# The first tile's norm weights, applied per partition behind the transposes instead of along the rows ahead of them

## The chip, the cores and the metric

The kernel runs on one core of a Trainium2 chip. The metric is the device time of one launch in microseconds (us). The core has five engines that work side by side, each through its own instructions in order: TensorE (PE in the profile; its weight loads are PEld), VectorE (DVE), ScalarE (ACT), GpSimd (POOL) and SyncE (SP), which here issues nearly all the transfers (DMAs). They wait for each other by semaphores.

## What is computed

One layer with 512 rows of 1024 features. The input is normalized, multiplied by its weights `norm_mix_pre` and projected by `w_in`; the projections feed a recurrence and a sparse attention, and a feed-forward net follows. All of the change lies in the first two lines below and in the first columns of `z`.

```python
def rmsnorm(x, g):
    x32 = x.astype(jnp.float32)
    y = x32 * lax.rsqrt(jnp.mean(x32 * x32, axis=-1, keepdims=True) + NORM_EPS)
    return (y * g.astype(jnp.float32)).astype(x.dtype)

h = rmsnorm(x, norm_mix_pre[i])
z = h @ w_in[i]
xr, gr, q, kc, vc, ksl, vsl, kw, vw, g_nsa, gm_rnn, gm_attn = jnp.split(z, IN_SPLITS, axis=-1)
```

## The kernel before

Every 32-bit product is made of three: each operand is split into a high half that TensorE reads in one pass (`fp32r`) and the low rest, and high x high, high x low and low x high are summed in PSUM. ScalarE makes the high half (a cast), VectorE the low one (a subtraction). A split of a weight block is therefore one DMA, one cast and one subtraction.

The 512 rows are four tiles of 128. For each, `x_load` fetches the rows; ScalarE sums the squares; VectorE makes mean plus epsilon, GpSimd raises it to the power -0.5 (`rstd`), and VectorE multiplies the rows by it and by the weights `g_pre`, which stand as one row of 1024 in all 128 partitions (`xn`). `to_T` (L228) then turns `xn` on TensorE, eight blocks of 128x128, four to a PSUM bank, and splits each bank as a whole into `aTh` (ScalarE, L237) and `aTl` (VectorE, L238), features on the partitions.

`v_unit(t, br)` (L325) multiplies tile t by the weights `VWh`/`VWl`: 8 steps of 128 features, three matmuls each, so 24 matmuls of 256 columns (`br` 0, the unit's PSUM tile is `mm`) or of 304 (`br` 1, `sc`). The weights of `br` 0 come as two blocks of 2 steps (`vw_first`, tiles `raw`) and one of 4 steps (`vw_parts[0]`, staged in `y`), those of `br` 1 as four of 2 steps (also in `y`). `VP` lists which of these four are subtracted on GpSimd instead of VectorE. In the middle of the units stand the transposes of the next tile: `TV` says behind how many steps; for the first tile it is 12, that is behind 4 steps of the second unit.

For the first tile all is done by halves of 512 columns (`norm1_halves`, L300), and `g_pre` is made on the core: `spread` (L367) multiplies a column of ones by the weights' row (`g_row`, one partition, 4 KB), and ScalarE copies the two products into `g_pre`. `keep_warm(n)` (L362) issues n matmuls of 512 columns on a constant tile (`warm`), whose result nobody reads; `WARM` gives their numbers at four places: ahead of the product, behind it, and behind each half of the transposes.

Behind the units come the projections: `f_raw(n)` (L142) issues the DMA of weight block n (512 KB, tile `raw`), `f_split(n)` (L148) its cast (`wh`) and subtraction (`wl`). Blocks 0, 1 and 2 are loaded in the loop over the tiles (L405), blocks 0 and 1 split there too (L409); the split of block 2 is called for in the middle of the first projection (`proj_k`, L177), and nothing but the scheduler says where it goes.

The order of each engine's instructions is made by a scheduler, which sorts by its own estimates of when operands are there; TensorE's is kept as written (`strict`). `keep_in_program_order` and `issue_after` bind it at single places. The transfers are issued by SyncE and run one behind the other through 16 DMA engines.

Of the kernel before, what the change touches and what calls it, by code (L numbers as in the profile page):

```python
# [8 lines left out]
F32 = mybir.dt.float32  # L9
F32R = mybir.dt.float32r  # L10
BF16 = mybir.dt.bfloat16
AF = mybir.ActivationFunctionType
# [19 lines left out]
PRO = (22, 5, 0, 0, 1, 12, 4, 3)  # L32
TK = (1, 7, 1)
TV = (12, 7, 8, 11)
VP = (4,)
WARM = (7, 2, 1, 3)


def f32(ap):
    return ap.bitcast(F32)  # L40
# [3 lines left out]
def layer_kernel(ctx, tc, a, out):  # L44
# [18 lines left out]
    def bank(tag, shape=None):  # L63
        return ps.tile(shape or [128, 512], F32, tag=tag, name=nm(tag), bufs=PB[tag])
# [24 lines left out]

    def pe(ins):  # L90
        return tc.keep_in_program_order(ins) if strict[0] else ins

    def mm(*args, **kw):
        return pe(nc.tensor.matmul(*args, **kw))  # L94

    def tp(*args):
        return pe(nc.tensor.transpose(*args))  # L97
# [108 lines left out]
            next(filler[0], None)  # L206


    slcol = const.tile([128, NG], F32, name="slcol")
    for h in range(NH):  # L210
        nc.gpsimd.memset(slcol[32 * (h % 4):32 * (h % 4) + 32, h // 4:h // 4 + 1], SLOPE[h])
    ident = const.tile([128, 128], F32, name="ident")
    make_identity(nc, ident)
    mhalf = const.tile([128, 1], F32, name="mhalf")
    nc.gpsimd.memset(mhalf, -0.5)

# [8 lines left out]
        last["pow"] = nc.gpsimd.tensor_tensor(r, r, mhalf, op=OP.pow)  # L225
        return r

    def to_T(src, t, tag, then=None):  # L228

        for b in range(2):  # L230
            pt = bank(tag)
            for j in range(4):
                k = 4 * b + j
                tp(pt[:, j * 128:(j + 1) * 128], src[:, k * 128:(k + 1) * 128], ident)
            v = pt.rearrange("p (j q) -> p j q", j=4)
            oh = aTh[:, 4 * b:4 * b + 4, t * 128:(t + 1) * 128]
            last["Th"] = nc.scalar.copy(oh, v)  # L237
            last["Tl"] = nc.vector.tensor_sub(aTl[:, 4 * b:4 * b + 4, t * 128:(t + 1) * 128], v, f32(oh))  # L238
            if then:
                then(b)  # L240

    def bcast_row(pool, src, tag, bufs):
        g = pool.tile([128, D], F32, tag=tag, name=nm(tag), bufs=bufs)
# [33 lines left out]

    def vw_first(k, ks, w):
        raw = wraw(w_in[:, k:k + ks, C_VSL:C_VSL + 256], [128, ks, 256], w, 0)
        nc.scalar.copy(VWh[:, k:k + ks, 0:256], raw)  # L280
        nc.vector.tensor_sub(VWl[:, k:k + ks, 0:256], raw, f32(VWh[:, k:k + ks, 0:256]))

    def vw_load(parts):
        for c0, src, n, k, ks in parts:
# [9 lines left out]
    def x_load(t, parts=(slice(0, D),)):  # L294
        v = e1.tile([128, D], F32, tag="x", name=nm("x"), bufs=3)
        for c in parts:
            nc.sync.dma_start(v[:, c], a["x"][0, t * 128:(t + 1) * 128, c])
        return v

    def norm1_halves(v, then):  # L300
        xn = e1.tile([128, D], F32, tag="xn", name=nm("xn"))
        ss = e1.tile([128, 2], F32, tag="ss2", name=nm("ss"), bufs=1)
        for u, c in enumerate(HALF):
            nc.scalar.activation(xn[:, c], v[:, c], AF.Square, accum_out=ss[:, u:u + 1])
        then()
        r = e1.tile([128, 1], F32, tag="rstd", name=nm("rstd"), bufs=4)
        nc.vector.tensor_scalar(ss[:, 0:1], ss[:, 0:1], 1.0 / D, EPS, op0=OP.mult, op1=OP.add)
        nc.vector.scalar_tensor_tensor(r, ss[:, 1:2], 1.0 / D, ss[:, 0:1], op0=OP.mult, op1=OP.add)
        last["pow"] = nc.gpsimd.tensor_tensor(r, r, mhalf, op=OP.pow)
        for c in HALF:  # L310
            last["xn"] = nc.vector.scalar_tensor_tensor(xn[:, c], v[:, c], r, g_pre[:, c], op0=OP.mult, op1=OP.mult)
        return xn

    def norm1_sum(v):
        xn = e1.tile([128, D], F32, tag="xn", name=nm("xn"))
        ss = e1.tile([128, 1], F32, tag="ss", name=nm("ss"), bufs=4)
        nc.scalar.activation(xn, v, AF.Square, accum_out=ss)
        return v, xn, ss
# [34 lines left out]

    warm = e1.tile([128, S], BF16, name="warm", bufs=1)
    nc.vector.memset(warm, 1.0)
    ones = e1.tile([1, 128], F32, name="ones", bufs=1)
    nc.vector.memset(ones, 1.0)
    g_row = e1.tile([1, D], F32, name="g_row", bufs=1)
    nc.scalar.dma_start(g_row, a["norm_mix_pre"][0:1, :])
    g_pre = e1.tile([128, D], F32, name="gpre", bufs=1)  # L360

    def keep_warm(n):  # L362
        p_ = bank("sc")
        for i in range(n):
            mm(p_, warm[:, 0:128], warm, start=(i == 0), stop=(i == n - 1))

    def spread():  # L367
        keep_warm(WARM[0])
        pg = [bank("mm") for c in HALF]
        for c, p_ in zip(HALF, pg):  # L370
            mm(p_, ones, g_row[:, c], start=True, stop=True)
        keep_warm(WARM[1])
        for c, p_ in zip(HALF, pg):
            nc.scalar.copy(g_pre[:, c], p_)

    x0 = x_load(0, HALF)
    xn = norm1_halves(x0, spread)
    pow0 = last["pow"].ins
    with tc.issue_after(last["xn"].ins):
        vw_first(0, 2, "a")  # L380
    to_T(xn, 0, "tr", lambda b: keep_warm(WARM[2 + b]))
    with tc.issue_after(last["xn"].ins):
        vw_first(2, 2, "b")
    early = ExitStack()
    early.enter_context(tc.issue_after(last["Th"].ins))
    early.enter_context(tc.issue_after(last["Tl"].ins))
    vw_load(vw_parts[:1])
    xv = {1: norm1_sum(x_load(1))}
    vw_load(vw_parts[1:])

    def turn_next(t):
# [970 lines left out]
```

## Time and profile before

| | |
|---|---|
| median of 3 runs | 933.45 us (933.41 to 933.84) |
| the profiled execution, its own time | 935.22 us |
| its span, first to last instruction | 933.2 us |
| TensorE busy (PE) | 914.7 us, 98% of the span |
| VectorE (DVE) | 619.7 us, 66% |
| ScalarE (ACT) | 478.9 us, 51% |
| GpSimd (POOL) | 131.2 us, 14% |
| DMA, mean over the span | 101 GB/s |
| DMA in the first of 40 slices (0 to 23 us) | 279 GB/s |

Busy shares are means over stages with different limits. TensorE is nearly always busy, so a change in the first 25 us is read from the order of events there: which wait ends last ahead of a stretch without holes. In a chain or a timeline each line has the start in us, the length in us, the engine, the line of the kernel and what is written from what; a bracket at the end gives the idle time just before and the engine or DMA that ended it. Matmuls are pipelined, so of a row of them the distance of the starts is the price, not the length of one.

### The profile page before, as it was taken

To read this page: it belongs to the slowest core of one execution; us is meant where nothing else is said; L and a number is where in the kernel's file an instruction comes from. 1 tells how busy PE (TensorE), PEld (TensorE's weight loads), DVE (VectorE), ACT (ScalarE), POOL (GpSimd) and SP (SyncE) were. 2 spreads that over 40 slices of the span, in tenths; PEclk is the share of its full clock that TensorE was granted. 3 is DMA by queue.
4 is the path that set the end of the run, shared out by engine and by line. 5 is a ranking of instruction groups with operands and counts; after the bars stand their busy time and mean duration, and the time that the engine had idled before them with its cause. 6 is when DMAs were issued, how large, how long until landed. Compare 5 with 4: busy or idle time off the path is not lost.

```text
span 933.2 us, 12423 instructions
## 1 busy us (share of the span) xinstructions
PE 914.7 (98%) x4496; PEld 754.8 (81%) x4496; DVE 619.7 (66%) x1198; ACT 478.9 (51%) x878; POOL 131.2 (14%) x214
## 2 busy tenths in 40 slices
PE   8999999999999999999999999999999999989998
PEld 5988888878878878878788988888888888777786
DVE  6657785968788888787847444434334478988933
ACT  6456947566667767666745322232223244555610
POOL 4001201123243223333302000000000000000100
PEclk9999999999999999999999999999999999999999
DMA  9224344362123111201136133333333345516401
GB/s 279 79 75 123 97 121 128 95 132 68 46 55 82 46 46 46 68 27 65 65 133 187 48 89 90 102 102 91 95 108 91 92 147 199 190 61 218 166 34 46
DMA packets 123999, 94.04 MB, mean 101 GB/s; under 512 B 6081, under 2 KB 107297, under 8 KB 123938
## 3 DMA queue, kind: packets, MB, share of 16 engines
q1 hardware_dynamic: 122784, 91.16, 32.3%
q0 software_dynamic: 1152, 2.10, 1.4%
q8 instruction: 35, 0.57, 0.2%
q14 instruction: 26, 0.21, 0.1%
q10 hardware_dynamic: 2, 0.00, 0.0%
HBM read 89.05 MB, written 2.10 MB: 98 GB/s over the span
## 4 chain that ended last, share of the span: by engine, by line
PE 86%; DVE 9%; ACT 3%; issue 2%; POOL 0%; DVEq 0%; ACTq 0%
PE mm L94 44%; PE sc L94 23%; PE mq L94 6%; PE pv L94 5%; PE tr L94 5%; PE tr L97 4%; DVE e L787 1%; DVE PT L871 1%; DVE wl L156 1%; ACT e L790 1%; PE sc L97 1%; DVE att L901 1%; ACT wh L155 0%; DVE pc L852 0%; DVE r L600 0%
## 5 line engine op out<-in xcount | busy, mean ns | idle before, releaser
L94 PE MATMUL mm<-aTh,wh 128*128 128x512 f32 (+1 forms) x536 | 211.8, 395 | 0.6 <-ACT st L1105 0.6
L94 PE MATMUL mm<-aTh,wl 128*128 128x512 f32 (+1 forms) x536 | 206.2, 385 | 0.1
L94 PE MATMUL mm<-aTl,wh 128*128 128x512 f32 (+1 forms) x536 | 206.0, 384 | 0.2 <-DVE aTl L238 0.2
L94 PEld LDWEIGHTS mm<-aTh,wl 128*128 128x128 f32 x536 | 100.8, 188 | 20.9 <-DVE wl L156 0.5
L94 PEld LDWEIGHTS mm<-aTh,wh 128*128 128x128 f32 x536 | 100.8, 188 | 19.3 <-issue 2.7
L84 ACT CAST wh<-raw 128x1024 fp32r<-128x1024 f32 x43 | 45.3, 1054 | 135.2 <-PE mm L94 58.1
L94 PEld LDWEIGHTS mm<-aTl,wh 128*128 128x128 f32 x536 | 101.1, 189 | 16.4 <-DVE aTl L238 0.5
L802 POOL TENSOR_SCALAR e<-e,sm 128x128 f32<-128x128 f32 (+3 forms) x128 | 80.0, 641 | 153.8 <-DVE sm L798 107.4
L85 DVE TENSOR_TENSOR wl<-raw,wh 128x1024 fp32r<-128x1024 f32 x43 | 52.6, 1223 | 68.1 <-ACT wh L84 62.8
L156 DVE TENSOR_TENSOR wl<-raw,wh 128x1024 fp32r<-128x1024 f32 x59 | 73.6, 1248 | 30.7 <-ACT wh L155 29.8
L790 ACT ACTIVATE e<-e,mn 128x128 f32<-128x128 f32 (+3 forms) x128 | 71.3, 558 | 25.9 <-DVE mn L787 19.0
L94 PE MATMUL sc<-aTh,wh 128*128 128x512 f32 (+1 forms) x208 | 79.3, 381 | 0.0
L155 ACT CAST wh<-raw 128x1024 fp32r<-128x1024 f32 x59 | 61.9, 1050 | 34.0 <-PE mm L94 30.0
L94 PE MATMUL sc<-aTh,wl 128*128 128x512 f32 (+1 forms) x208 | 79.2, 381 | 0.0
L94 PE MATMUL sc<-aTl,wh 128*128 128x512 f32 (+1 forms) x208 | 79.2, 381 | 0.0
L787 DVE CUSTOM_DVE_ANT_0 e<-sc,toep 128x128 f32<-128x128 f32 (+3 forms) x128 | 59.5, 483 | 17.3 <-PE sc L94 16.4
L871 DVE TENSOR_TENSOR PT<-tr,PT 128x512 fp32r<-128x512 f32 x96 | 56.5, 596 | 15.4 <-ACT PT L870 14.4
L870 ACT CAST PT<-tr 128x512 fp32r<-128x512 f32 x96 | 47.5, 509 | 26.0 <-PE tr L97 25.3
L991 POOL TENSOR_TENSOR ss<-ss,ss 128x1 f32<-128x1 f32 x8 | 4.6, 577 | 392.6 <-ACT junk L979 392.6
L94 PE MATMUL sc<-KS,QS 128*128 128x512 f32 (+2 forms) x192 | 54.6, 366 | 1.1 <-DVE mn L787 1.0
L97 PE MATMUL tr<-ident,e 128*128 128x128 f32 x320 | 49.3, 273 | 2.9 <-DVE c L821 2.0
L97 PEld LDWEIGHTS tr<-ident,e 128*128 128x128 f32 x320 | 39.6, 140 | 13.0 <-PE tr L97 2.6
(360 smaller groups left out, 1762.4 us busy)
## 6 DMA issues: line engine op xcount, KB each, us to landing
raw<-in_w_in_dram SPq DMA_DIRECT2D x48, 512.0 KB, 3.6
raw<-in_ffn_w_gate_up_dram SPq DMA_DIRECT2D x44, 512.0 KB, 3.7
raw<-in_ffn_w_down_dram SPq DMA_DIRECT2D x30, 512.0 KB, 4.1
raw<-in_ple_w_gate_dram SPq DMA_DIRECT2D x8, 512.0 KB, 4.0
x<-in_x_dram SPq DMA_DIRECT2D x7, 512.0 KB, 7.0
raw<-in_w_out_dram SPq DMA_DIRECT2D x6, 512.0 KB, 3.6
raw<-in_cmp_k_w_dram SPq DMA_DIRECT2D x4, 512.0 KB, 3.7
raw<-in_cmp_v_w_dram SPq DMA_DIRECT2D x4, 512.0 KB, 3.9
```

The lines of the kernel that those rows point to most:

```text
L84: nc.scalar.copy(h, raw)
L85: nc.vector.tensor_sub(l, raw, f32(h))
L94: return pe(nc.tensor.matmul(*args, **kw))
L97: return pe(nc.tensor.transpose(*args))
L155: nc.scalar.copy(h, RAW[n])
L156: nc.vector.tensor_sub(l, RAW[n], f32(h))
L787: nc.vector.tensor_tensor_reduce(e[:, br, :], src, toep[:, 384 - 128 * i:S], SLOPE[h], BIG, op0=OP.add, op1=OP.min, accum_out=mn[:, u, br: ...
L790: tt(nc.scalar.activation(e[:, br, :], e[:, br, :], AF.Exp, scale=-1.0, bias=mn[:, u, br:br + 1], accum_out=sm[:, u, br:br + 1]))
L802: nc.gpsimd.tensor_scalar(ev, ev, sm[:, v, br:br + 1], 1.0, op0=OP.mult, op1=OP.mult)
L870: nc.scalar.copy(P[:, 0, :2 * n], pt[:, :2 * n])
L871: nc.vector.tensor_sub(P[:, 1, :2 * n], pt[:, :2 * n], f32(P[:, 0, :2 * n]))
L901: last["cl_dve"] = nc.vector.tensor_add(att[64 * u:64 * u + 64, half * 256:half * 256 + 256], pv[0:64, u, :], tmp[:, u, :])
```

## The change

The first tile's `xn` is now `x` times `rstd` alone (a `tensor_scalar` per half). The weights are loaded as eight rows of 128 (`g_rows`), turned by one transpose into a column per step (`g_col`, 128 partitions x 8), and applied where the turned tile leaves PSUM: `first_T` casts and subtracts each of the eight 128x128 blocks by itself, with that step's column as a scale per partition. `spread`, `ones` and `g_row` are gone. The constant matmuls stand at two places, 7 and 6 (`WARM = 13`), ahead of the transposes. The other tiles still use `g_pre`, which is now a broadcast load of 512 KB (`bcast_row`), issued behind the load of the second tile. `VP` is empty: all four subtractions of `br` 1 are VectorE's. `ident` is made ahead of `slcol`.

```diff
-VP = (4,)
-WARM = (7, 2, 1, 3)
+VP = ()
+WARM = 13
...
-            last["xn"] = nc.vector.scalar_tensor_tensor(xn[:, c], v[:, c], r, g_pre[:, c], op0=OP.mult, op1=OP.mult)
+            last["xn"] = kept(nc.vector.tensor_scalar(xn[:, c], v[:, c], r, None, op0=OP.mult))
...
-    g_row = e1.tile([1, D], F32, name="g_row", bufs=1)
-    nc.scalar.dma_start(g_row, a["norm_mix_pre"][0:1, :])
-    g_pre = e1.tile([128, D], F32, name="gpre", bufs=1)
+    g_rows = e1.tile([KT, 128], F32, name="g_rows", bufs=1)
+    nc.scalar.dma_start(g_rows, a["norm_mix_pre"][0].rearrange("(k p) -> k p", p=128))
+    g_col = e1.tile([128, KT], F32, name="g_col", bufs=1)
...
-    def spread():
-        keep_warm(WARM[0])
-        pg = [bank("mm") for c in HALF]
-        for c, p_ in zip(HALF, pg):
-            mm(p_, ones, g_row[:, c], start=True, stop=True)
-        keep_warm(WARM[1])
-        for c, p_ in zip(HALF, pg):
-            nc.scalar.copy(g_pre[:, c], p_)
+    def first_T(src):
+
+        for b in range(2):
+            pt = bank("tr")
+            for j in range(4):
+                k = 4 * b + j
+                tp(pt[:, j * 128:(j + 1) * 128], src[:, k * 128:(k + 1) * 128], ident)
+            for j in range(4):
+                k = 4 * b + j
+                v, oh = pt[:, j * 128:(j + 1) * 128], aTh[:, k, 0:128]
+                last["Th"] = kept(nc.scalar.activation(oh, v, AF.Copy, scale=g_col[:, k:k + 1]))
+                last["Tl"] = kept(nc.vector.scalar_tensor_tensor(aTl[:, k, 0:128], v, g_col[:, k:k + 1], f32(oh),
+                                                                 op0=OP.mult, op1=OP.subtract))
+            if b == 0:
+                vw_first(2, 2, "b")
 
     x0 = x_load(0, HALF)
-    xn = norm1_halves(x0, spread)
+    keep_warm(WARM - 6)
+    pg = bank("tr")
+    tp(pg[:, :KT], g_rows, ident[:KT, :KT])
+    kept(nc.vector.tensor_copy(g_col, pg[:, :KT]))
+    xn = norm1_halves(x0)
     pow0 = last["pow"].ins
+    keep_warm(6)
     with tc.issue_after(last["xn"].ins):
         vw_first(0, 2, "a")
-    to_T(xn, 0, "tr", lambda b: keep_warm(WARM[2 + b]))
-    with tc.issue_after(last["xn"].ins):
-        vw_first(2, 2, "b")
+        first_T(xn)
...
     xv = {1: norm1_sum(x_load(1))}
+    g_pre = bcast_row(e1, a["norm_mix_pre"][0], "gpre", 1)
     vw_load(vw_parts[1:])
```

Three places of the order that follows from it. ScalarE, from the first tile's transposes on, before (`L237` casts a bank of the turned tile, `L288` weights staged in `y`, `L317` sums squares, `L332` and `L335` take a unit's result, `L155` casts a projection's weight block; `wh61_592` is block 2's):

```order
L237 CAST aTh_91<-tr10_161 128x4x128
L237 CAST aTh_91<-tr12_170 128x4x128
L288 CAST VWh_117<-y_96 128x4x256
...
L317 ACTIVATE xn22_251,ss23_252<-x21_249 128x1024
L237 CAST aTh_91<-tr24_254 128x4x128
L237 CAST aTh_91<-tr25_261 128x4x128
...
L332 CAST V_106<-mm26_283 128x4x64
L155 CAST wh61_592<-raw46_476 128x1024
```

And now (`L374` casts one block of 128 columns with its scale, `L239` is the cast of a bank, `L157` that of a projection's block; `wh59_599` is block 2's; brackets name the semaphores waited for):

```order
L374 ACTIVATE aTh_91<-tr9_160,g_col_124 128x128 [waits DVE_49,PE_49]
L374 ACTIVATE aTh_91<-tr9_160,g_col_124 128x128 [waits DVE_49] x3
L280 CAST VWh_117<-raw10_173 128x2x256 [waits DMAHW4_49]
L374 ACTIVATE aTh_91<-tr11_177,g_col_124 128x128 [waits PE_49]
L374 ACTIVATE aTh_91<-tr11_177,g_col_124 128x128 [waits DVE_49] x3
L288 CAST VWh_117<-y_96 128x4x256 [waits DMAHW5_49]
...
L316 ACTIVATE xn20_258,ss21_259<-x19_256 128x1024 [waits DMAHW4_49]
L157 CAST wh59_599<-raw44_483 128x1024 [waits DMAHW0_49]
L239 CAST aTh_91<-tr22_261 128x4x128 [waits PE_49]
```

Two casts of a bank have become eight of a block, the later ones with a wait for VectorE, and the cast of block 2 has moved from behind the second tile's first unit to ahead of the second tile's transposed halves.

VectorE, from the weights of the second unit to the second tile's low halves, before:

```order
L290 TENSOR_TENSOR VWl_118<-y_96,VWh_117 128x2x304 x2
L322 SCALAR_TENSOR_TENSOR xn16_190<-x15_188,rstd20_245,gpre_126 128x1024
L290 TENSOR_TENSOR VWl_118<-y_96,VWh_117 128x2x304
L333 TENSOR_TENSOR V_106<-mm18_205,V_106 128x4x64
L224 TENSOR_SCALAR rstd27_305<-ss23_252 128x1
L322 SCALAR_TENSOR_TENSOR xn22_251<-x21_249,rstd27_305,gpre_126 128x1024
L238 TENSOR_TENSOR aTl_92<-tr24_254,aTh_91 128x4x128
```

and now:

```order
L290 TENSOR_TENSOR VWl_118<-y_96,VWh_117 128x2x304 [waits DMAHW3_49,Activation_49]
L332 TENSOR_TENSOR V_106<-mm16_212,V_106 128x4x64 [waits Activation_49]
L321 SCALAR_TENSOR_TENSOR xn13_195<-x12_193,rstd18_252,gpre15_198 128x1024 [waits DMAHW7_49,DMAHW6_49,Pool_49]
L226 TENSOR_SCALAR rstd25_312<-ss21_259 128x1 [waits Activation_49]
L158 TENSOR_TENSOR wl60_600<-raw44_483,wh59_599 128x1024 [waits DMAHW0_49,Activation_49]
L321 SCALAR_TENSOR_TENSOR xn20_258<-x19_256,rstd25_312,gpre15_198 128x1024 [waits DMAHW4_49,Pool_49]
L240 TENSOR_TENSOR aTl_92<-tr22_261,aTh_91 128x4x128 [waits Activation_49]
```

The second tile's `xn` has moved behind all four weight subtractions and the first unit's V, and block 2's subtraction to ahead of the second tile's `aTl`.

SyncE, the issues of the transfers from the load of the second tile on, now:

```order
L297 DMA x_193<-in_x_dram 128x1024
L244 DMA gpre_198<-in_norm_mix_pre_dram 128x1024
L287 DMA y<-in_w_in_dram 128x2x304 x4
L297 DMA x_256<-in_x_dram 128x1024
L297 DMA x_316<-in_x_dram 128x1024
L148 DMA raw_340<-in_w_in_dram 128x8x128
L148 DMA raw_397<-in_w_in_dram 128x8x128
L148 DMA raw_483<-in_w_in_dram 128x8x128
L429 DMA prow<-in_conv_w_dram 32x128
```

The broadcast (`gpre`) is new, and block 2 (`raw_483`) stands ahead of four loads for the recurrence (`y` from `lru_wa` and `lru_wx`), two of which were ahead of it.

## Rows read from the trace of the kernel before

**Rows 1.** The page: the chain that ended last, shares of the span by engine

```profile
PE 86%; DVE 9%; ACT 3%; issue 2%; POOL 0%; DVEq 0%; ACTq 0%
```

**Rows 2.** Waits of TensorE, 20 to 130 us: total, times, longest us

```profile
PE mm L94 <- DVE aTl L238: 0.6, 1, 0.6
```

**Rows 3.** The chain, 20 to 45 us: start us, length us, what

```profile
22.30 2.51 PE mm L94 x19
...
29.39 2.84 PE mm L94 x24
...
42.76 2.33 PE mm L94 x10
```

**Rows 4.** Windows: stretch, length, busy PE PEld DVE ACT POOL, clock, DMA share, GB/s

```profile
0.00:12.00 12.00, 10.55 (x24) 4.52 (x25) 4.24 (x9) 6.06 (x12) 6.37 (x32) 1.00 0.83 283
12.00:14.00 2.00, 2.00 (x12) 1.84 (x11) 1.67 (x2) 2.00 (x5) 0.00 (x0) 1.00 1.04 409
14.00:16.00 2.00, 2.00 (x18) 2.00 (x18) 1.65 (x4) 2.00 (x5) 1.66 (x3) 1.00 1.10 326
16.00:18.00 2.00, 1.56 (x12) 1.32 (x10) 2.00 (x2) 1.75 (x4) 2.00 (x2) 1.00 1.20 288
```

**Rows 5.** DMA issues at 16.7 and at 464.2 us: count, KB, us to landing

```profile
raw<-in_w_in_dram SPq DMA_DIRECT2D x1, 512.0 KB, 7.0
...
g<-in_norm_mix_post_dram SPq DMA_DIRECT2D x1, 512.0 KB, 8.8
```

**Rows 6.** Groups by form, whole span: count, busy us, mean ns, idle before

```profile
L155 ACT CAST wh<-raw 128x1024 fp32r<-128x1024 f32 x59 | 61.9, 1050 | 34.0 <-PE mm L94 30.0 <-PE sc L94 3.8
...
L544 ACT COPY KC<-tr 128x124 f32<-128x124 f32 x1 | 0.2, 243 | 0.0
...
L790 ACT ACTIVATE e<-e,mn 128x128 f32<-128x128 f32 x32 | 12.6, 395 | 5.6 <-DVE mn L787 5.4
...
L821 DVE SCALAR_TENSOR_TENSOR c<-ctab,tr 128x128 f32<-128x128 f32 x16 | 3.5, 278 | 0.3 <-PE tr L97 0.3
```

**Rows 7.** Timeline, 1 to 22 us: start, length, engine, line, operation

```profile
1.45 3.17 PE L94 MATMUL sc<-warm 128*128 128x512 bf16 x7 [1.45 <-DVE warm L355]
...
6.19 0.55 POOL L309 TENSOR_TENSOR rstd<-rstd,mhalf 128x1 f32<-128x1 f32 x1 [2.67 <-DVE rstd L308]
...
8.98 0.75 DVE L311 SCALAR_TENSOR_TENSOR xn<-x,rstd,gpre 128x512 f32<-128x512 f32 x1 [0.88 <-ACT gpre L374]
...
12.08 0.69 DVE L238 TENSOR_TENSOR aTl<-tr,aTh 128x512 fp32r<-128x512 f32 x1 [0.54 <-ACT aTh L237]
...
13.02 1.23 DVE L290 TENSOR_TENSOR VWl<-y,VWh 128x1024 fp32r<-128x1024 f32 x1 [0.25 <-ACT VWh L288]
...
14.66 1.49 DVE L290 TENSOR_TENSOR VWl<-y,VWh 128x608 fp32r<-128x608 f32 x2 [0.35 <-ACT VWh L288]
...
15.60 0.28 PE L94 MATMUL mm<-VWh,aTl 128*128 128x256 f32 x1
...
16.07 2.53 DVE L322 SCALAR_TENSOR_TENSOR xn<-x,rstd,gpre 128x1024 f32<-128x1024 f32 x1
...
18.66 1.10 PE L97 MATMUL tr<-ident,xn 128*128 128x128 f32 x8 [1.09 <-DVE xn L322]
...
19.23 0.41 DVE L333 TENSOR_TENSOR V<-mm,V 128x256 fp32r<-128x256 f32 x1
...
20.36 1.28 DVE L322 SCALAR_TENSOR_TENSOR xn<-x,rstd,gpre 128x1024 f32<-128x1024 f32 x1 [0.67 <-POOL rstd L225]
...
21.57 1.28 DVE L238 TENSOR_TENSOR aTl<-tr,aTh 128x512 fp32r<-128x512 f32 x2
```

**Rows 8.** Windows of TensorE alone: stretch, length, PE busy, clock, DMA share, GB/s

```profile
17.30:18.60 1.30, 0.26 (x2) 1.00 1.25 246
...
816.40:818.90 2.50, 0.06 (x1) 1.00 0.16 62
818.90:822.30 3.40, 3.39 (x8) 0.50 0.48 154
```

More of the change, by code (lines that the diff above doesn't have):

```diff
@@ L91, in pe @@
         return tc.keep_in_program_order(ins) if strict[0] else ins
+    kept = tc.keep_in_program_order
     def mm(*args, **kw):
@@ L206, in fill @@
             next(filler[0], None)
+    ident = const.tile([128, 128], F32, name="ident")
+    make_identity(nc, ident)
     slcol = const.tile([128, NG], F32, name="slcol")
@@ L211, in layer_kernel @@
         nc.gpsimd.memset(slcol[32 * (h % 4):32 * (h % 4) + 32, h // 4:h // 4 + 1], SLOPE[h])
-    ident = const.tile([128, 128], F32, name="ident")
-    make_identity(nc, ident)
     mhalf = const.tile([128, 1], F32, name="mhalf")
@@ L226, in rstd_of, with to_T @@
         return r
-    def to_T(src, t, tag, then=None):
+    def to_T(src, t, tag):
         for b in range(2):
@@ L238, in to_T @@
             last["Tl"] = nc.vector.tensor_sub(aTl[:, 4 * b:4 * b + 4, t * 128:(t + 1) * 128], v, f32(oh))
-            if then:
-                then(b)
     def bcast_row(pool, src, tag, bufs):
@@ L279, in vw_first @@
         raw = wraw(w_in[:, k:k + ks, C_VSL:C_VSL + 256], [128, ks, 256], w, 0)
-        nc.scalar.copy(VWh[:, k:k + ks, 0:256], raw)
-        nc.vector.tensor_sub(VWl[:, k:k + ks, 0:256], raw, f32(VWh[:, k:k + ks, 0:256]))
+        kept(nc.scalar.copy(VWh[:, k:k + ks, 0:256], raw))
+        kept(nc.vector.tensor_sub(VWl[:, k:k + ks, 0:256], raw, f32(VWh[:, k:k + ks, 0:256])))
     def vw_load(parts):
@@ L298, in x_load, with norm1_halves @@
         return v
-    def norm1_halves(v, then):
+    def norm1_halves(v):
         xn = e1.tile([128, D], F32, tag="xn", name=nm("xn"))
@@ L304, in norm1_halves @@
             nc.scalar.activation(xn[:, c], v[:, c], AF.Square, accum_out=ss[:, u:u + 1])
-        then()
         r = e1.tile([128, 1], F32, tag="rstd", name=nm("rstd"), bufs=4)
@@ L355, in layer_kernel @@
     nc.vector.memset(warm, 1.0)
-    ones = e1.tile([1, 128], F32, name="ones", bufs=1)
-    nc.vector.memset(ones, 1.0)
-    g_row = e1.tile([1, D], F32, name="g_row", bufs=1)
-    nc.scalar.dma_start(g_row, a["norm_mix_pre"][0:1, :])
-    g_pre = e1.tile([128, D], F32, name="gpre", bufs=1)
+    g_rows = e1.tile([KT, 128], F32, name="g_rows", bufs=1)
+    nc.scalar.dma_start(g_rows, a["norm_mix_pre"][0].rearrange("(k p) -> k p", p=128))
+    g_col = e1.tile([128, KT], F32, name="g_col", bufs=1)
     def keep_warm(n):
```

## The prediction

> **What bounds the kernel now.** First the chain of work that ended last: TensorE holds 86% of it [rows 1], so what counts is when TensorE can go on and at which clock. Then what TensorE waits for once it has started: from 20 to 130 us there is one wait of any size, 0.6 us for `aTl`, the low halves of the second tile [rows 2]. The chain in order of time shows where it ends: at 22.30 us, at the third matmul of the second tile's first unit; behind it transposes, units of 24 matmuls and projections follow each other without a hole [rows 3]. From here on the order of the instructions is the same in both kernels, apart from the third weight block named below. So I treat 22.30 as a gate: what moves it moves the end by as much, and nothing behind it gives the time back. Ahead of it the question is which chain reaches the gate last.
>
> **The queue of transfers: the third weight block.** In the changed order ScalarE stands at the cast of weight block 2 (`wh<-raw`, third of the `f_raw` blocks) before it may cast the second tile's transposes, and VectorE stands at that block's subtraction (`wl`) and at the third tile's normalization before the second tile's `aTl`. Both engines work in order, so the second tile now waits for the landing of that block. Up to the second block the kernel before moves 5312 KB (two halves of `x`, 512; two first weights, 512; `y` 512; `x` 512; four parts of 304; `x` twice, 1024; two blocks, 1024), that is 5.44 MB. The windows give 12 x 283 + 2 x 409 + 2 x 326 + 2 x 288 = 5.44 MB by 18.0 us [rows 4]: the queue is full all the way, and the second block is in at 18.0 at the earliest. The change puts two loads of 0.52 MB before the end of the third block: the broadcast of the norm weights, which goes ahead of the four `y` parts, and the block itself, now ahead of the small loads. At 409 for the first and 288 for the second, the rates of the windows with the like rows, that is 1.3 + 1.8 us: 21.1. The small loads between 18 and 20 us mix in, and a landing is told a little behind the last byte; I take 22.0. The bounds: 20.6, if both go at 409 from 18.0; 23.7, the landing of the same block in the kernel before, issued at 16.7 and in 7.0 us later [rows 5].
>
> From 22.0: the cast takes 1.05, a subtraction of that size 1.23, the third tile's normalization 1.28, half of `aTl` 0.69 [rows 6, 7]. Neighbours on VectorE overlap by some 0.07 (a normalization started at 20.36, took 1.28, and the next start was at 21.57), so 22.0 + 1.05 + 1.16 + 1.21 + 0.69 = 26.1, and with two hops of about 0.04 the gate opens at 26.2. **That is 3.9 us later**; by the bounds 2.5 to 5.6.
>
> **The first tile: what is gained and spent there.** Removed: the product of ones and `g_row`, on whose copies the halves of `xn` waited, the second until 8.98 us, so that it ended at 9.73 [rows 7]. Now both follow the power on GpSimd, which ends at 6.74 [rows 7]: two of at most 0.75 end by 8.2, and the first half, which the transposes wait for first, by 7.5. TensorE has 6 more constant matmuls of 0.45 to do from 4.6 on, until 7.3, and its transposes end near 8.5. Gain: some 2 us. Spent: the cast and the subtraction go by 128 columns with a scale per partition, and the order shows ScalarE's second to fourth piece with a wait on VectorE: each piece alternates with the other engine's. No such piece is in the trace. A copy of 124 columns from PSUM takes 0.24 on ScalarE, an exponential of 128 columns with a per-partition operand 0.40; 128 columns with a PSUM operand take 0.28 on VectorE [rows 6]. With two hops of 0.04 to 0.09 a pair lasts 0.60 to 0.86; I take 0.75, since the scale is read per partition. Eight pairs and one weight subtraction in between end at 8.5 + 6.0 + 0.35 = 14.9, where the last `aTl` was done at 12.77 [rows 7]. The cast of `y` (1.05, from ScalarE's last piece on, 0.3 earlier) and its subtraction (1.23) follow only then: 16.9, and 12 matmuls of 0.118 [rows 3] end the first unit at 18.3; it ended at 15.9 [rows 7].
>
> The Trainium skill, page "PSUM — Partial Sum Buffer", section "PSUM bank collisions raise a hardware error", says that ScalarE and VectorE must not touch one bank in the same partitions at once, reads included. The trace agrees as far as it goes: the order of the pieces in both kernels has that wait. By that rule the eight pairs cost 6.0; if both engines could read the bank at once they would cost some 3, and the first unit would end near 15.3.
>
> Then VectorE: the subtraction that GpSimd did now stands here too, four of 0.72 in a row (two took 1.49, overlap taken off), the low half of V 0.41 less that overlap, `xn` of the second tile 1.28: 16.9 + 2.9 + 0.35 + 1.28 = 21.4. `VP = ()` gives something back: that `xn` took 2.53 while GpSimd subtracted, against 1.28 elsewhere [rows 7]. The eight transposes of the second tile (1.10) end at 22.5, where they ended at 19.8 [rows 7]. ScalarE is held by block 2 until 23.1, so this chain has 0.6 us to spare: **the first tile's balance costs nothing as long as the block lands behind 21.4**. Cover gone, it would cost what the first rival says.
>
> **The clock.** TensorE runs at 1.2 GHz at the start (7 matmuls of 512 columns in 3.17 us) [rows 7] and at 2.4 when a unit takes 2.84 [rows 3]. Near the end of the kernel the granted clock fell to 0.50 behind 2.5 us with 0.06 busy, and stayed there for 3.4 us; a hole of 1.3 us at 17.3 left it at 1.00 [rows 8]. In the changed kernel TensorE has the transposes done at 22.5, the 12 matmuls that are left of its unit (a half of the 24) some 1.6 later, two matmuls to do on the second tile, and waits until 26.2: a hole of 2.0, nearer to 2.5 than to 1.3. And in the first unit it has three matmuls per pair of 0.75 us. 3.4 us at half speed cost 1.7; part of it may lie in the hole. I take 1.2, bounds 0 and 1.7.
>
> **Sum.** 3.9 + 1.2 = 5.1 us. The profiled execution took 935.22 (span 933.2, 2.0 around it), 1.8 above the median of the runs; what changes lies inside the span, so I add to the median: 933.45 + 5.1 = **938.5**.
>
> **Rivals.**
> 1. Not slower by what can be told (0.2%, 1.9 us, is about that): block 2 lands before ScalarE needs it. Place: ScalarE's cast ahead of the second tile's. It decides at a landing before some 20.5, which needs the broadcast to cost nearly nothing. Then the gate is set by the first tile: second tile's transposes at 22.5, the unit's other 12 matmuls to 24.1, two of the next, gate at 24.3: +2.0, and with pairs of 0.60 some 1.2 less: +0.8. Time 934.2 to 935.4. For it: the queue reached 409 [rows 4]; against it: 1.05 MB more in a queue that was full until 18.0. Faster than before would need pairs under 0.5 as well, below the sum of the two durations of rows 6.
> 2. The clock stays: +3.9, 937.3. For it the hole of 1.3 us that left the clock alone; two matmuls stand in the new one.
> 3. The broadcast is slow: the same kind of load took 8.8 us from issue to landing at 464 us [rows 5], behind another block in the queue. If its bytes move at half of 409, +1.3: 939.8, and with the whole 1.7 of the clock 940.3.
> 4. The constant matmuls don't do what the title says, and the clock is still 1.2 GHz at the first transposes: the transposes are then as slow as before, which the 8.5 has in it already. Time as forecast.
>
> **How the numbers follow.** Forecast with the clock falling (rival 4 in it) 0.50; rival 2 0.22; rival 3 0.10; rival 1 0.10; faster 0.03; slower than all of them (both holes slow, block near 23.7) 0.05. The range 935.8 to 940.9 leaves out rival 1, faster, and the last. The first bound is the landing at 20.6 without the clock (+2.5), the upper the slow load with the clock's whole price and some. Faster by over 0.2%: 0.03; within: 0.10; slower: 0.87.
>
> **What would show it.** Right: ScalarE idle ahead of `wh<-raw` with that DMA as the releaser, its start at 21 to 23.7 us; the second tile's `aTl` at 25 to 27; TensorE's longest hole just ahead of it; ScalarE and VectorE alternating on `g_col` at 0.60 to 0.86 a pair; the first projection (42.76 before [rows 3]) at 46.6 to 48. Wrong: the cast of block 2 starting without idle time, or a hole of TensorE late in the kernel that shrank by the same time, or the gate at 22 us.

## The result, and the profile after

The changed kernel is slower: 939.82 us, median of four runs (937.51 to 942.61), against 933.64 of the kernel before beside it, a ratio of 1.006 (95% 1.0043 to 1.0077). Timed once more it had 940.31 (five runs, 939.57 to 942.19) against 933.82 (29 runs), a ratio of 1.0069 (1.0057 to 1.0081). The forecast was 938.5, the range 935.8 to 940.9, and slower by over 0.2% had 0.87.

The chain of the changed kernel, first execution (937.51 us, span 935.7), from 12 to 48 us; start, length, what:

```profile
12.85 9.55 DMA raw<-in_w_in_dram
...
22.42 1.06 ACT wh L157
...
25.84 0.70 DVE aTl L240
...
26.58 2.50 PE mm L96 x19
...
33.68 2.84 PE mm L96 x24
...
47.05 12.96 PE mm L96 x57
```

A transfer now stands in the chain ahead of the gate, and it is block 2 (`raw`, whose cast is L157); before, the chain went there through VectorE's `xn` and `aTl`. The gate has moved from 22.30 to 26.58, the first projection from 42.76 to 47.05: 4.28 and 4.29 us. From the gate to the first projection it takes what it took (20.46 before, 20.47 now). The waits from 5 to 60 us (engine, line, waited for: total, times, longest) name the links:

```profile
ACT aTh L374 <- DVE aTl L375: 3.1, 6, 0.8
...
ACT wh L157 <- DMA raw<-in_w_in_dram: 2.0, 1, 2.0
...
PE mm L96 <- DVE aTl L240: 1.7, 1, 1.7
```

The 0.6 us that TensorE waited for `aTl` [rows 2] are 1.7. The first line is the other thing that was forecast: six of the first tile's pieces on ScalarE wait for VectorE's piece before them. The timeline shows both stretches (start, length, engine, line, operation, in brackets idle time before and its releaser):

```profile
6.83 1.12 PE L99 MATMUL tr<-ident,xn 128*128 128x128 f32 x8 [0.49 <-DVE xn L310]
...
9.33 0.37 ACT L374 ACTIVATE aTh<-tr,g_col 128x128 fp32r<-128x128 f32 x1 [0.42 <-DVE aTl L375]
9.74 0.35 DVE L375 SCALAR_TENSOR_TENSOR aTl<-tr,g_col,aTh 128x128 fp32r<-128x128 f32 x1 [0.44 <-ACT aTh L374]
10.12 0.37 ACT L374 ACTIVATE aTh<-tr,g_col 128x128 fp32r<-128x128 f32 x1 [0.42 <-DVE aTl L375]
...
13.99 0.35 DVE L375 SCALAR_TENSOR_TENSOR aTl<-tr,g_col,aTh 128x128 fp32r<-128x128 f32 x1 [0.43 <-ACT aTh L374]
14.92 1.23 DVE L290 TENSOR_TENSOR VWl<-y,VWh 128x1024 fp32r<-128x1024 f32 x1 [0.58 <-ACT VWh L288]
...
18.95 0.37 ACT L331 CAST V<-mm 128x256 fp32r<-128x256 f32 x1 [0.62 <-PE mm L96]
...
19.71 1.28 DVE L321 SCALAR_TENSOR_TENSOR xn<-x,rstd,gpre 128x1024 f32<-128x1024 f32 x1
...
21.75 1.21 PE L99 MATMUL tr<-ident,xn 128*128 128x128 f32 x8
22.42 1.05 ACT L157 CAST wh<-raw 128x1024 fp32r<-128x1024 f32 x1 [2.05 <-DMA raw<-in_w_in_dram]
23.37 1.06 ACT L239 CAST aTh<-tr 128x512 fp32r<-128x512 f32 x2
23.50 1.23 DVE L158 TENSOR_TENSOR wl<-raw,wh 128x1024 fp32r<-128x1024 f32 x1 [2.45 <-ACT wh L157]
24.64 1.28 DVE L321 SCALAR_TENSOR_TENSOR xn<-x,rstd,gpre 128x1024 f32<-128x1024 f32 x1
25.84 1.28 DVE L240 TENSOR_TENSOR aTl<-tr,aTh 128x512 fp32r<-128x512 f32 x2
```

ScalarE's pieces start 0.79 us apart, each in the idle time of the other engine's. The second tile's transposes (21.75) come 3.1 us later than before [rows 7] and are done at 22.96; ScalarE, idle for 2.05 us until block 2 has landed at 22.42, casts that block first. The transposes did not wait for the normalized rows, which were done at 20.99, but for TensorE, which had matmuls of its units to finish until then.

TensorE's clock in the first units (length, busy PE, PEld, DVE, ACT, POOL, clock, DMA share, GB/s):

```profile
12.00:14.00 2.00, 1.16 (x5) 0.86 (x5) 0.71 (x3) 1.15 (x4) 0.00 (x0) 0.50 1.08 411
...
20.00:22.00 2.00, 2.00 (x10) 1.97 (x10) 1.05 (x2) 0.37 (x2) 0.55 (x1) 0.50 1.26 240
22.00:24.00 2.00, 2.00 (x17) 2.00 (x16) 0.50 (x1) 1.58 (x3) 0.00 (x0) 0.97 1.17 154
```

From 11.9 to 22.1 us the granted clock is 0.50, that is 1.2 GHz, even where TensorE is busy without a break; behind the hole at the gate it stays at 2.4 in this execution, and it does not fall near 820 us either, as it did in the profiled execution of before [rows 8]. So the two profiled executions differ by 4.29 us at the first projection but by 2.3 in time: behind it before has 890.4 us to go and this one 888.7.

### The profile page after: what moved, and what is told of

Read it like the earlier page. It is cut to its first block, busy times and chain, and to the rows that moved or that the text cites. A ratio compares the mean times of both kernels' runs of the same rounds, so it can differ in the third digit from the quotient of the medians.

```text
span 935.7 us, 12426 instructions
## 1 busy us (share of the span) xinstructions
PE 912.5 (98%) x4493; PEld 754.6 (81%) x4493; DVE 619.6 (66%) x1205; ACT 479.5 (51%) x882; POOL 131.2 (14%) x213
## 4 chain that ended last, share of the span: by engine, by line
PE 84%; DVE 9%; ACT 3%; issue 2%; DMA 1%; POOL 0%; SPq 0%; DVEq 0%; ACTq 0%; POOLq 0%
PE mm L96 43%; PE sc L96 22%; PE mq L96 6%; PE pv L96 5%; PE tr L96 5%; PE tr L99 3%; DVE PT L879 1%; DVE e L795 1%; DMA raw<-in_w_in_dram 1%; DVE wl L158 1%; ACT e L798 1%; ACT wh L157 1%; PE sc L99 1%; DVE att L909 1%; DVE pc L860 0%
## 5 line engine op out<-in xcount | busy, mean ns | idle before, releaser
L96 PEld LDWEIGHTS mm<-aTh,wh 128*128 128x128 f32 x536 | 100.9, 188 | 19.3 <-issue 2.7
L157 ACT CAST wh<-raw 128x1024 fp32r<-128x1024 f32 x59 | 61.8, 1049 | 35.7 <-PE mm L96 29.7
L795 DVE CUSTOM_DVE_ANT_0 e<-sc,toep 128x128 f32<-128x128 f32 (+3 forms) x128 | 59.5, 484 | 17.4 <-PE sc L96 16.7
L878 ACT CAST PT<-tr 128x512 fp32r<-128x512 f32 x96 | 47.7, 510 | 26.2 <-PE tr L99 25.6
```

What stands on the lines that cost most here:

```text
L157: nc.scalar.copy(h, RAW[n])
L795: nc.vector.tensor_tensor_reduce(e[:, br, :], src, toep[:, 384 - 128 * i:S], SLOPE[h], BIG, op0=OP.add, op1=OP.min, accum_out=mn[:, u, br: ...
L878: nc.scalar.copy(P[:, 0, :2 * n], pt[:, :2 * n])
```

## The experiments

Each kernel was timed beside the kernel before. This table is worked out from their traces: start of block 2's cast (where the second tile's turned halves stand behind it), start of the first projection in the chain, what is left of the span from there, and where the granted clock was 0.50. Each row is one execution. (The first matmul in a timeline starts 0.22 us ahead of the chain's row; expectations that name 42.55, 44.72 or 41.45 count from that one.)

| kernel | cast | first projection | rest | clock at 0.50, us |
|---|---|---|---|---|
| before | | 42.76 | 890.4 | 819 to 822 |
| changed, first trace | 22.42 | 47.05 | 888.7 | 12 to 22 |
| changed, second trace | 23.39 | 49.57 | 888.9 | 11 to 22, 28 to 32 |
| block 2 split late | | 44.94 | 889.1 | 11 to 21 |
| pieces from two banks | | 41.67 | 891.0 | 12 to 15, 817 to 821 |
| no broadcast load | 20.84 | 45.47 | 889.1 | 12 to 22 |
| hole at the gate filled | 22.88 | 47.51 | 890.6 | 12 to 22, 824 to 828 |
| late split, first unit filled | | 44.27 | 888.8 | 17 to 20 |
| late split, no constant matmuls | | 45.43 | 890.3 | 821 to 825 |
| before, VP empty | | 40.21 | 890.3 | 8 to 11, 817 to 820 |
| reordered | | 40.07 | 889.1 | none while TensorE works |

What is left behind the first projection is 888.7 to 889.1 without a fall of the clock near 820 us and 890.3 to 891.0 with one. The question is therefore only the start and the clock.

**Block 2 split late.** It undoes the one move that the forecast's largest term rests on.

```diff
-        if k == 2:
+        if k == 2 and n == 0:
+            with tc.issue_after(last["Th"].ins), tc.issue_after(last["Tl"].ins):
+                f_split(2)
+        elif k == 2:
             f_split(n + 2)
```

> The changed kernel, with the split of weight block 2 (cast and subtraction) put behind the last split of a turned tile, so that neither ScalarE nor VectorE meets it ahead of the second tile's turned halves. Theory: in the changed kernel the gate (third matmul of the second tile's first unit, 26.58 us, hole of 1.98 us ahead of it) waits for that block's landing. Without it the hole closes to under 0.3 us and the gate falls to where TensorE itself arrives, 24.6 to 24.9; the first projection, at 47.05 in the changed kernel and at 42.76 before, starts at 45.0 to 45.4. What stays of the shift (some 2.4 us) is the first tile's. Rival A (the first tile is covered, as the prediction had it): nothing of the shift stays, first projection at 43 to 43.5. Rival B (the block is not what is waited for, only the wait's name): first projection stays at 46.8 to 47.2, the hole with it.

Measured: 937.09 us (935.02 to 939.24), ratio 1.0021 (1.0011 to 1.0031). The chain at the gate:

```profile
22.80 1.67 PE sc L96 x12
24.48 2.50 PE mm L96 x21
27.84 0.35 PE mm L96 x3
...
44.94 15.23 PE mm L96 x67
```

The hole is gone: 21 matmuls in a row where 19 stood behind it. The first projection is 2.11 us earlier. So block 2 holds half of the 4.29; the other half is the first tile's, hidden as long as the block is late. That is what the prediction's first rival gives for this case (+2.0); rival A above, put down there to the prediction, is not what it says, for its first tile costs nothing only while the block is late.

**No broadcast load.** `g_pre` is a memset of ones on GpSimd in place of `bcast_row`, so the kernel leaves out the norm weights of the second to fourth tile.

> The changed kernel without the broadcast load of the norm weights: g_pre is filled with ones, so the weights of the second to fourth tile are left out of the result. 0.52 MB less go through the queue ahead of weight block 2. Theory: the block's cast, which waited for the landing until 22.42 us, starts 1.0 to 1.5 us earlier (20.9 to 21.4), and the gate and the first projection move by as much as TensorE lets them, to 45.6 to 46.1. Rival A (the queue is not full there, the load is hidden): the cast starts at 22.2 to 22.5 as before, no change. Rival B (the broadcast runs at half the rate of other loads): 2 us or more earlier at the cast.

Measured: 937.92 us (936.34 to 938.39), ratio 1.0034 (1.0023 to 1.0046). Block 2's cast in its timeline, and the first of the four loads for the recurrence:

```profile
20.84 1.05 ACT L157 CAST wh<-raw 128x1024 fp32r<-128x1024 f32 x1 [0.30 <-DMA raw<-in_w_in_dram]
...
20.89 0.72 SPq L343 DMA_DIRECT2D y<-in_lru_wa_dram  x1
```

The same load in the changed kernel:

```profile
18.73 0.72 SPq L343 DMA_DIRECT2D y<-in_lru_wa_dram  x1
```

The cast starts 1.58 us earlier than in the first trace with the load (2.55 earlier than in the second), and the first projection follows by the same 1.58. So the queue is full there, and bytes ahead of the block delay it. But the 1.58 is not the broadcast's alone (1.3 in the forecast): without it the four loads for the recurrence, 128 KB each, also go out behind the block's landing, where in the changed kernel they go out ahead of it and share the queue. What each of the two gives is not separated. The runs lie within 2.05 us, those of the changed kernel within 5.1 and 2.6.

**The hole at the gate filled.** Nine constant matmuls (`keep_warm(9)`) ahead of the second tile's first unit.

> The changed kernel with nine more matmuls of 512 columns on the constant tile (0.21 us each, 1.9 in all) between the first tile's last unit and the second tile's first, in the time in which TensorE waits for block 2's chain; the gate should stay within 0.3 us of 26.58. Theory: the runs of the changed kernel differ by up to 5 us (937.51 to 942.61) because TensorE's clock falls in some of them behind this hole and the sparse first unit; the hole filled, the times draw together at 937.3 to 938.5. Rival A: the falls come elsewhere (in the first unit, or near the end of the kernel); the times spread as before, 937.5 to 942. Rival B: the nine matmuls themselves push the gate, and the first projection starts over 0.5 us later than 47.05.

Measured: 939.86 us (938.25 to 941.39), ratio 1.0049 (1.0035 to 1.0063). The narrow band that was expected did not come: in the trace the clock stays up behind the gate and falls near 824 us instead. Since it also stayed up in the first trace of the changed kernel, without the fill, these runs don't tell what the fill is worth.

**The changed kernel again.**

> The changed kernel itself, once more, to see how its runs spread and what a second execution shows. Theory: two things vary between its runs, the landing of weight block 2 (22.42 us in the first trace, 22.88 in the one with the filled hole) and TensorE's clock in the hole of 2.85 us near 820 us, which all kernels here have: where the clock falls behind it a run is 1.7 to 2.3 us longer. So the times lie at 937.3 to 938.3 or at 939.2 to 940.5, a landing later still adds its delay, and in a trace the first projection follows the cast of block 2 by 24.4 us. Rival (the clock falls behind the hole at the gate in the longer runs, as the prediction had it): the trace of a longer run shows half clock between 25 and 30 us, and the first projection follows the cast by over 25 us.

The theory of a fall near 820 us fails in this execution (940.31 us), and the rival holds, a fall behind the gate as the prediction had it. Block 2 is cast at 23.39, the gate opens at 27.54 behind holes of 0.9 and 2.4 us, and the first projection follows the cast by 26.2. From its chain:

```profile
23.39 1.05 ACT wh L157
...
27.54 3.77 PE mm L96 x19
```

Windows of half a microsecond show the clock:

```profile
27.00:27.50 0.50, 0.00 (x0) 0.00 (x0) 0.50 (x2) 0.00 (x0) 0.00 (x0) 1.00 0.58 132
27.50:28.00 0.50, 0.46 (x3) 0.46 (x4) 0.50 (x1) 0.00 (x0) 0.00 (x0) 1.00 0.58 109
28.00:28.50 0.50, 0.50 (x6) 0.50 (x5) 0.47 (x3) 0.05 (x1) 0.00 (x0) 0.86 0.88 223
28.50:29.00 0.50, 0.50 (x5) 0.50 (x4) 0.00 (x0) 0.15 (x1) 0.45 (x1) 0.50 1.13 339
...
31.50:32.00 0.50, 0.50 (x6) 0.50 (x5) 0.00 (x0) 0.00 (x0) 0.00 (x0) 0.73 0.00 0
```

It falls some 0.8 us behind the hole and stays down for 3.4 us. From gate to first projection it is now 22.03 us, against 20.47 in the first execution: the fall costs 1.56. The gate itself is 0.96 later than in the first execution, with the block's landing (0.97).

**Pieces from two banks.** All eight transposes first; then the pieces alternate between the two PSUM banks. The second weight split, which stood between the fourth and the fifth pair, comes behind all of them.

```diff
-            for j in range(4):
-                k = 4 * b + j
-                v, oh = pt[:, j * 128:(j + 1) * 128], aTh[:, k, 0:128]
+        for j in range(4):
+            for b in range(2):
+                k = 4 * b + j
+                v, oh = pts[b][:, j * 128:(j + 1) * 128], aTh[:, k, 0:128]
```

> The changed kernel, with the first tile's eight transposes ahead of all its pieces, and the pieces taken from the two PSUM banks in turn, so that ScalarE casts in one bank while VectorE subtracts in the other; the second weight split stands behind the pieces. The scheduler by itself puts the split of block 2 behind the second tile's casts, so the hole at the gate should go too, as in the kernel with the late split. Theory: a pair costs 0.78 us because the two engines take turns in one bank (0.37 and 0.35, one behind the other). In turn between banks a piece of either engine follows the next at 0.37 to 0.45, the last low half of the first tile ends at 11.2 to 12.0 instead of 14.34, the first unit ends 1.5 to 2.5 earlier than 18.7, and the first projection starts at 42.5 to 44.0. Rival (the engines do not work side by side for another reason, such as each piece's own hand-over): the pair stays above 0.7, and the first projection starts at 45 or later as with the late split alone.

Measured: 934.44 us (933.70 to 934.94), ratio 0.9996 (0.9988 to 1.0005): the loss is gone. The pieces in its timeline, now two of either engine in a row:

```profile
9.36 0.63 ACT L377 ACTIVATE aTh<-tr,g_col 128x128 fp32r<-128x128 f32 x2 [0.16 <-DVE aTl L378]
9.76 0.61 DVE L378 SCALAR_TENSOR_TENSOR aTl<-tr,g_col,aTh 128x128 fp32r<-128x128 f32 x2 [0.18 <-ACT aTh L377]
10.14 0.63 ACT L377 ACTIVATE aTh<-tr,g_col 128x128 fp32r<-128x128 f32 x2 [0.16 <-DVE aTl L378]
...
17.13 1.28 DVE L321 SCALAR_TENSOR_TENSOR xn<-x,rstd,gpre 128x1024 f32<-128x1024 f32 x1
```

Two pieces each in 0.78 us where one went before: 0.39 a pair. The eight pairs end at 11.15 instead of 14.34 (of the 3.2 us some 0.3 is the weight split's place), the first projection starts at 41.67, 3.27 ahead of the late split alone and 5.4 ahead of the changed kernel. The Trainium skill, page "PSUM — Partial Sum Buffer", section "PSUM bank collisions raise a hardware error", says that the two engines must not touch one bank in the same partitions at once. The two traces agree in so far as the engines never do: the program's semaphores keep them apart, and that costs 0.79 a pair from one bank and 0.39 from two. What the chip does without the semaphores no run here shows. Block 2's split went behind the second tile's casts in this kernel, so the 5.4 holds the gain of the late split too; and the clock is back up at 15 us instead of 21, so the 3.27 holds what that gives.

**The first unit's clock.** The late split, and six constant matmuls each ahead of the first unit's third and fifth step.

> The changed kernel with the late split of block 2, and twice six matmuls on the constant tile in the first tile's first unit, ahead of its third and its fifth step, where TensorE stands 1.7 and 2.2 us. Theory: the granted clock is 0.50 from 11.9 to 22.1 us because TensorE does little from 9.4 us on; with the two holes filled it stays at 1.00, the second tile's transposes wait for its normalized rows (done at 21.2) instead of TensorE, and start at 21.2 to 21.4 instead of 21.96: the first projection starts at 43.9 to 44.2 instead of 44.72, and the runs are 0.5 to 0.9 us shorter than with the late split alone. Rival A (the clock costs nothing here, VectorE's chain sets the transposes): first projection at 44.6 to 44.8 with the clock at 1.00. Rival B (the clock falls all the same, in the hole inside the fifth step): the constant matmuls then take 0.42 us each and the first unit ends up to 1 us later.

Measured: 936.60 us (934.91 to 936.97), ratio 1.0023 (1.0015 to 1.0032). The second tile's transposes:

```profile
21.05 1.09 PE L99 MATMUL tr<-ident,xn 128*128 128x128 f32 x8
```

The clock is at 0.50 from 16.6 to 20.0 us only, the transposes come 0.7 us earlier (21.77 with the late split alone) and wait for the normalized rows, and the first projection is 0.67 earlier. So the part of the low clock that went costs 0.7 us once block 2 is out of the way. The times (1.0023 against 1.0021) can't tell that.

**VP empty, alone.** `VP = ()` in the kernel before.

> The kernel before with one part of the change, VP empty: all four subtractions of the second branch on VectorE. In its order four subtractions and the low half of V now stand ahead of the second tile's normalization, where two stood. Theory: 1.4 us more of subtractions and 0.4 of V ahead of it, 1.25 less for the normalization itself, which ran 2.53 us beside GpSimd's subtraction and should run 1.28: the second tile's transposes start 0.3 to 0.7 us later than 18.66, and the first projection at 42.9 to 43.3 (42.55 before). Rival A (the normalization was slow for another reason): it still takes 2.5, and the transposes come 1.6 to 1.9 us later. Rival B (only what GpSimd did counts): 0.3 to 0.6 us earlier.

Measured: 935.10 us (932.70 to 935.50), ratio 1.0004 (0.9995 to 1.0012): no difference that the times show. The normalization of the second tile takes 1.28, not 2.53, as the theory had it, but stands later in VectorE's row. The profiled execution, with 932.7 us the shortest, shows another thing:

```profile
4.50 1.98 PE L94 MATMUL mm<-g_row,ones 1*128 1x512 f32 x4
...
15.67 1.28 DVE L322 SCALAR_TENSOR_TENSOR xn<-x,rstd,gpre 128x1024 f32<-128x1024 f32 x1
```

In the profiled execution of before the same product took nearly twice as long:

```profile
4.55 3.78 PE L94 MATMUL mm<-g_row,ones 1*128 1x512 f32 x4
```

In this execution with the empty VP the product's four matmuls take half the time, as they would at twice the clock; the granted clock then was 0.50 from 8 us on for 3.4. The first projection is 2.55 earlier than before, where 0.35 to 0.75 later was expected. The product alone ends 1.85 us earlier, so this trace can't say what VP is worth at the first projection.

**No constant matmuls.** The late split without the 7 and the 6 of `WARM`.

> The changed kernel with the late split of block 2 and without its thirteen matmuls on the constant tile. Theory: TensorE is then at 1.2 GHz at the first tile's transposes, which take 0.26 us each instead of 0.14; the first bank is turned 0.5 us later, and all that follows on ScalarE and VectorE shifts by that: first projection at 45.0 to 45.4 instead of 44.72, time 0.3 to 0.7 above the kernel with the late split alone. Rival A: nothing, since VectorE's row of work sets the first 20 us. Rival B: the clock stays at 1.2 GHz longer than to 22 us, and the second tile is late as well: 46 or more.

Measured: 936.94 us (935.47 to 939.26), ratio 1.0029 (1.0018 to 1.0040), which the times can't tell from the late split. In the trace the first tile's eight transposes go at 1.2 GHz, and the first projection is 0.49 later:

```profile
6.99 1.97 PE L99 MATMUL tr<-ident,xn 128*128 128x128 f32 x8 [3.12 <-DVE xn L313]
```

From its chain, the two halves of the first tile's second unit, on either side of the second tile's transposes:

```profile
19.30 3.04 PE sc L96 x12
...
23.30 1.68 PE sc L96 x12
```

**Reordered.** Two banks, late split, the second weight split between the second and third pair of each bank, eight constant matmuls ahead of the fifth step, and two of the four subtractions behind the second tile's normalization:

```diff
+            lows.append((VWl[:, k:k + ks, c0:c0 + n], raw, f32(VWh[:, k:k + ks, c0:c0 + n])))
+            if c0 == 0 or k < 4:
+                kept(nc.vector.tensor_sub(*lows.pop()))
...
             xn = norm1(*xv.pop(t + 1))
             if t == 0:
+                kept(last["xn"])
+                while lows:
+                    kept(nc.vector.tensor_sub(*lows.pop(0)))
```

> The changed kernel with three things put otherwise: the first tile's pieces in turn from two banks (with the second weight split in the middle of them), block 2's split late, and of the four subtractions of the second branch the two that the transposes do not need put behind the second tile's normalization; eight matmuls on the constant tile ahead of the first unit's fifth step. Theory (VectorE's row of work ahead of the second tile's transposes is what sets the gate once pieces and block are out of the way): the normalization starts at 15.4 to 15.8 instead of 17.13, the transposes at 16.7 to 17.2 instead of 18.46, and the first projection at 39.6 to 40.4, against 41.45 with two banks alone and 42.55 before: the time is 1.0 to 1.8 us below the two-bank kernel and below that of before. Rival (TensorE or the transfers set it by then): the first projection stays at 41 to 41.5.

Measured: 932.79 us (930.51 to 933.70), ratio 0.9980 (0.9971 to 0.9989): faster than both kernels, than the kernel before by 0.2%. The rows that set it:

```profile
15.46 1.28 DVE L326 SCALAR_TENSOR_TENSOR xn<-x,rstd,gpre 128x1024 f32<-128x1024 f32 x1
...
16.80 1.09 PE L99 MATMUL tr<-ident,xn 128*128 128x128 f32 x8
...
18.40 1.28 DVE L243 TENSOR_TENSOR aTl<-tr,aTh 128x512 fp32r<-128x512 f32 x2
```

The normalization stands 1.67 us earlier in VectorE's row than with two banks alone, and the first projection follows by 1.60.

**The hole near 820 us filled**, in the reordered kernel and in the kernel before: seven matmuls into a free bank, between the two halves of the product that waits there. The scheduler then also puts the addition that is waited for one subtraction earlier.

```diff
         for t in range(2):
+            if t and fill:
+                p_ = bank("sc")
+                for i in range(fill):
+                    mm(p_, av[:, 0, 0:128], w[0][:, jj], start=(i == 0), stop=(i == fill - 1))
```

> The reordered kernel with seven matmuls of 512 columns, whose result nobody reads, in the hole of 2.85 us that TensorE has near 815 us (a wait for VectorE's adding up of a bank); the scheduler now also puts that bank's addition one block of subtractions earlier, so the hole itself is some 1.2 us shorter. Theory: the reordered kernel's runs fall into 930.5 to 931.0 (clock 0.999) and 932.2 to 933.7 (0.995 to 0.997), and the second group is the clock's fall behind this hole. With the hole filled all runs are at the lower group or below: 929.2 to 931.0, clock 0.999. Rival (the falls come from the first 30 us): two groups as before, at most shifted by the earlier addition.

> The kernel before with the same seven matmuls near 818 us and nothing else. Its runs lie in two groups, 933.1 to 934.2 and 934.9 to 935.6. Theory: the upper group is the fall behind this hole in runs whose start was slow, and it goes: all runs between 931.5 and 934.2. Compared with the reordered kernel that has the same seven matmuls, it is 1.5 to 3 us longer, which is what the start alone is worth. Rival: the groups stay, 2 us apart, with clock 0.995 to 0.998.

Measured: reordered 931.16 us (929.71 to 931.22), ratio 0.9964 (0.9952 to 0.9976); before 932.59 (930.45 to 934.25), 0.9976 (0.9963 to 0.9988). Both traces are without a fall, with 887.9 us behind the first projection instead of 889 or 890 to 891. Runs at a mean clock of 0.997 remain in both, so the expectation that all of them come together is not met; where the clock falls in those, no trace shows. What the seven matmuls and the earlier addition give by themselves is not separated. The start is worth 1.4 us between the two medians, a little under the 1.5 to 3 expected, and 2.76 between the two traces (first projection at 40.00 and 42.76).

## Why the prediction was right, and where it was off

- **What bounds the kernel.** Right. The gate moved, what stands behind it kept its length, and the shift carried to the end, but for the clock near 820 us.
- **Block 2.** Right in mechanism and nearly in size: gate +3.9 forecast, +4.28 and +5.24 measured in two executions. From the cast to the gate it is 4.16 and 4.15 us, where the sum had 4.2. The mis-sized step is the landing: 22.0 taken between bounds of 20.6 and 23.7, while the cast started at 22.42, 22.88 and 23.39 in three traces. What moves it from run to run stays open; without the broadcast, and with the loads for the recurrence behind it, it was 20.84.
- **The first tile.** Costs nothing as long as the block lands behind 21.4: right, and the late split shows the price without that cover, +2.18, where the first rival had +2.0. That rival puts the limit at 20.5 instead, which is nearer: with the cast at 20.84 (no broadcast load) the first projection is still 0.53 behind the late split's. Of its steps the pair was 0.79 (0.75 taken), the last `aTl` done at 14.34 (14.9) and the normalized rows at 20.99 (21.4). The first unit ended later than 18.3: V's cast, released by its last matmul, starts at 18.95. The step that failed is "12 matmuls of 0.118", which took the full clock where 0.50 was granted: the matmuls of that stretch stand 0.21 apart. With it the path is another: the second tile's transposes waited for TensorE and not for VectorE's row. That they were done at 22.96 for 22.5 is in part luck, an earlier row of VectorE against a slower TensorE. As to the banks, the order of the pieces in the kernel before has only VectorE's wait for the cast that it needs; ScalarE's wait for VectorE in one bank is new, and the eight pairs with the split between them take 6.8 us (6.35 taken), from 7.52 on instead of 8.5.
- **The clock.** 1.2 taken, as the likelier case; in the first execution it was 0, as in the second rival, and in the second 1.56. The hole was 1.98 us in the one and 2.35 with another 0.9 ahead in the other.
- **The sum.** 5.1 stood for a run with a landing at 22.0 and most of a fall. At the first projection the first execution is 4.29 later without a fall and the second 6.81 with one (49.57, behind the 46.6 to 48 that was to show it right); the medians are 6.2 and 6.5 above the kernel before. In the second execution the landing is 1.39 later than taken and the fall 0.36 dearer, which makes up the 1.7 over the 5.1; for the runs without a trace the split stays open.
- **The constant matmuls and VP.** The matmuls keep TensorE at 2.4 GHz for the first transposes (1.12 us, 1.97 without) and are worth 0.5 us in the trace and nothing that the times tell. VP empty shows no gain or loss in the times.

## What to carry to other kernels

A cast or subtraction whose weights are still in flight must not stand in an in-order engine's row ahead of work that another engine waits for: compare the landing with the place in the row, not only the durations. When two engines each read what the other reads from PSUM, let them take turns between two banks: here that halved the price of a pair. And compare executions by stretches (start of a marked step, rest of the span) before a few microseconds are put down to a change: here what is left behind the first projection is 1.2 to 2.3 us longer with a fall of TensorE's clock near 820 us, and the fall at the gate cost 1.56.

## What the runs showed of the hardware

- The granted clock reads 1.00 in the first microseconds of all these traces, while the constant matmuls of 512 columns, where a kernel has them there, stand 0.43 us apart; before the first recorded change only the distance of matmuls tells the clock. In the kernel before, matmuls of 256 columns stand 0.21 us apart until 13.3 us and 0.12 from there on, and the clock reads 1.00 all the while. Without the constant matmuls the record shows no fall before 821 us, but twelve matmuls of 304 columns take 3.04 us at 19.3 and 1.68 at 23.3.
- The start of a kernel that makes `g_pre` by a product is not always the same: the product takes 3.78 us in two traces (the kernel before, with and without the hole near 820 us filled) and 1.98 in the one with VP empty, as the clock rises behind or ahead of it. That trace and the kernel before's, both with a fall near 820 us, are 2.55 us apart at the first projection and 2.52 in time (932.70 and 935.22). That the kernel before itself has the early start in some runs is likely but not shown.
- The same hole of 2.45 us near 820 us (a wait for VectorE) stands in eleven traces. In five of them the clock fell there, in six it did not; what decides it these runs don't show.
- A fall need not come with the hole. In the second trace of the changed kernel TensorE was at work again for 0.8 us before the clock went down, and then for 3.4 us at half speed; with VP empty it fell some 1.1 us behind the end of the hole near 815 us, from two banks some 0.3 ahead of that end.
